# Two fused transformer blocks on one core: the modulation's loads and sums rearranged, the memory's keys and values moved beside the GLA projections, attention's last norms one step later

## The chip, the cores and the metric

The kernel runs on one core of a Trainium2 chip. TensorE (PE) multiplies matrices into PSUM banks; VectorE (DVE), ScalarE (ACT) and GpSimd (POOL) read and write SBUF and PSUM; 16 DMA engines move data between HBM and SBUF. Each engine executes its own list of instructions in order, and semaphores make one engine wait for another. The metric is the device time of one execution in microseconds (us); lower is better.

## The reference, cut to what matters

Two blocks run one after the other over a sequence of 1024 positions with 1024 channels, in fp32. The places that the change touches are the first norm and its modulation, the projections of gated linear attention (GLA), the keys and values of the cross-attention, and its last step with the norm behind it:

```python
# block 1
mod = silu(c) @ w_ada + b_ada                  # c: 1024 values, w_ada: 1024 x 6144
shift1, scale1, gate1, shift2, scale2, gate2 = split(mod, 6)
u = layer_norm(x) * (1 + scale1) + shift1      # x: 1024 x 1024
m = token_mixer(u, ...)                        # retention and GLA, w_in: 1024 x 3600
x = layer_norm(ALPHA*x + gate1*m, ...); u2 = layer_norm(x)*(1 + scale2) + shift2
x = layer_norm(ALPHA*x + gate2*(relu(u2 @ w_ff1)**2 @ w_ff2), ...)   # 4096 hidden channels
# block 2: a mixer of SSD, S5 and RG-LRU, then
k = mem @ wk; v = mem @ wv                     # mem: 256 x 1024, wk and wv: 1024 x 1024
o = softmax(q k^T / 16) v, 4 heads of 256; h = layer_norm(ALPHA*h1 + o @ wo, ln2)
# then an MLP with 4096 hidden channels and a last norm
```

## The kernel before, in words

The program is written as Python generators that are stepped beside each other: `weave(main, side, n)` steps `side` n times for each step of `main`, and `pipe` runs several generators one step behind each other. What they issue gets a fixed place on each engine at build time, so the order on every engine is set before the run.

**Products.** A matrix product in fp32 is made of three faster products (`mm3`, lines L114, L115, L116): each operand is kept as a rounded part `hi` (format fp32r) and the rest `lo`, and hi·hi, hi·lo and lo·hi are summed in PSUM. `split` makes the two parts: ACT casts (L82), DVE or POOL subtracts (L83). Weights are loaded into a staging page S and split into two pages each (`wpage`, `wcols`), with tag W by default. A page is 128 rows of 1024 values; there are U 4 (each four such pages wide), X 8, H 8, W 8, S 6.

**The start.** `kv_mem` transposes the two row tiles of `mem` on TensorE (L1080) and splits them into four X pages. `kv_proj` makes the cross-attention's keys (four steps of 256 columns, 48 products of 256 columns each) and values (two column halves, two steps each) and stores them to HBM; attention reads them some 1700 us later. `first_norm` loads x (four row tiles, then four more), normalises it, and has `mod_first` make scale1 and shift1: each needs eight row tiles of 128 x 1024 of w_ada. DVE adds six of them, each times its value of silu(c), into `acc` (L219, L221). TensorE then sums `acc` over its rows with one-column products against ones (L228, 8 of them), adds the last two row tiles directly (L230, 16 products against silu(c)), and DVE adds the bias (L233). Last, x is transposed on TensorE (L331, 64 transposes), scaled and shifted on the way out of PSUM, and split into the two parts of the page pair `T` (L341 subtracts). The main program steps `kv_proj` between the steps of `first_norm`, with POOL doing its weights' subtractions (`w_eng`).

**The GLA projections.** `gla_proj` reads T: 48 products give 16 gate channels, four fp32 products the gates (L404), then come four groups of 24 products of 512 columns for queries and four for keys (each copied out by ACT, L420), eight groups for values (ACT, L438) and eight for gates. Beside it, `early` makes the other four modulation vectors (`mods`: DVE sums w_ada tiles in X pages, in `mod_acc`, two of them summed by TensorE at L273 and finished by DVE at L274) and the constants of S5 (`s5_setup`, a long chain on DVE from L1420 on).

**The end of attention.** `attn_part(T, hd, h)` handles one head hd and one half h of the sequence in two steps: first queries, scores and the softmax, then the transposed probabilities (L1738), their product with the values, and the output projection added to the residual of each row tile. For the last head (hd == 3), each row tile is normalised at once, scaled (L171), stored as h2, transposed on TensorE (L182) and scaled and split for the MLP (ACT at L186). The MLP then starts with U pages as the left and W pages as the right operands; ACT finishes its first tiles at L772.

## Time and profile before

| | |
|---|---|
| three runs | 2683.71, 2690.9, 2692.58 us; median 2690.9 us |
| profiled execution | 2687.83 us, span of its trace 2686.1 us |
| mean granted clock of TensorE | 0.974 |
| TensorE busy | 2554.4 us, 95% of the span |
| VectorE, ScalarE, GpSimd busy | 1905.0, 1114.9 and 262.0 us (71%, 42%, 10%) |

The span is the stretch from the first to the last instruction that the trace holds; the rest of the execution's time lies around it. A busy time is the sum over one engine's instructions; TensorE's matrix products overlap in the records, so the distance from one start to the next is their real cost.

### The profile page before, as it was taken

Reading aid. Unit: us, or ns where it says so; the run is one execution under the profiler, and the core shown is the slowest. Engines: PE = TensorE matmul, PEld = TensorE weight load, DVE = VectorE, ACT = ScalarE, POOL = GpSimd, SP = SyncE. Lnnn points to the kernel's source line nnn. Section 1 sums busy time; section 2 is a strip of 40 time slices with the busy share of each in tenths; the row PEclk is TensorE's granted clock in tenths of the full one; section 3 lists DMA queues with packets and bytes.
Section 4 is the critical chain, followed back from the end, with each engine's and each line's share of the span. In section 5 each row is a group of like instructions: output and inputs, shape, how many; then the busy total and the mean of one; then the engine's idle time right before and its main releaser. Section 6 shows DMA issues by size and latency. Waiting matters only on the chain.

```text
span 2686.1 us, 32858 instructions
## 1 busy us (share of the span) xinstructions
PE 2554.4 (95%) x12086; PEld 2073.2 (77%) x12086; DVE 1905.0 (71%) x3237; ACT 1114.9 (42%) x1671; POOL 262.0 (10%) x238
## 2 busy tenths in 40 slices
PE   7899999889999999999999998999988999999997
PEld 7587777677888888888877776778867888888886
DVE  5858665778897777656965577785557787767759
ACT  3622233224654444433642572352246454434332
POOL 4121135530000000000001013100000000000000
PEclk8899999989999999999999998999998999999998
DMA  9772333454266568857632243361102756799763
GB/s 334 248 252 102 141 103 108 141 145 149 76 216 234 190 237 322 307 182 231 204 135 76 68 141 114 114 221 54 40 32 78 255 192 212 247 340 336 264 228 144
DMA packets 255129, 484.35 MB, mean 180 GB/s; under 512 B 21604, under 2 KB 110964, under 8 KB 254968
## 3 DMA queue, kind: packets, MB, share of 16 engines
q1 hardware_dynamic: 247768, 470.59, 51.7%
q10 hardware_dynamic: 7200, 11.67, 1.2%
q8 instruction: 95, 1.56, 0.2%
q14 instruction: 66, 0.54, 0.1%
HBM read 338.80 MB, written 143.38 MB: 180 GB/s over the span
## 4 chain that ended last, share of the span: by engine, by line
PE 75%; DVE 10%; ACT 4%; DMA 4%; issue 4%; POOL 3%; SPq 0%; POOLq 0%; DVEq 0%; ACTq 0%
PE ps L114 23%; PE ps L115 23%; PE ps L116 23%; ACT half L186 1%; DMA H<-r_qk 1%; PE ps L182 1%; DVE half L548 1%; DVE W L83 1%; DMA S<-in_xa_wk 1%; POOL X L527 1%; PE ps L540 1%; DVE st L155 1%; DMA H<-g_qkb 1%; POOL W L83 0%; DVE U L341 0%
## 5 line engine op out<-in xcount | busy, mean ns | idle before, releaser
L114 PE MATMUL ps<-U,W 128*128 128x512 f32 (+1 forms) x1080 | 426.1, 395 | 7.6 <-ACT ev L772 5.1
L114 PE MATMUL ps<-W,H 128*128 128x512 f32 x1088 | 425.1, 391 | 3.6 <-DVE sm L167 3.0
L115 PE MATMUL ps<-U,W 128*128 128x512 f32 (+1 forms) x1080 | 424.2, 393 | 1.5 <-DVE U L341 1.5
L115 PE MATMUL ps<-W,H 128*128 128x512 f32 x1088 | 423.9, 390 | 0.0
L116 PE MATMUL ps<-W,H 128*128 128x512 f32 x1088 | 423.9, 390 | 0.0
L83 DVE TENSOR_TENSOR W<-S,W 128x1024 fp32r<-128x1024 f32 (+1 forms) x272 | 330.2, 1217 | 131.6 <-ACT W L82 129.6
L116 PE MATMUL ps<-U,W 128*128 128x512 f32 (+1 forms) x1080 | 422.7, 392 | 0.8 <-DVE W L83 0.8
L82 ACT CAST W<-S 128x1024 fp32r<-128x1024 f32 x288 | 299.0, 1043 | 256.7 <-PE ps L115 175.6
L83 DVE TENSOR_TENSOR H<-S,H 128x1024 fp32r<-128x1024 f32 x130 | 158.5, 1220 | 154.2 <-ACT H L82 147.2
L82 ACT CAST H<-S 128x1024 fp32r<-128x1024 f32 x130 | 136.6, 1051 | 292.0 <-PE ps L115 226.1
L114 PEld LDWEIGHTS ps<-U,W 128*128 128x128 f32 (+1 forms) x1080 | 200.6, 186 | 57.5 <-ACT ev L772 5.4
L114 PEld LDWEIGHTS ps<-W,H 128*128 128x128 f32 x1088 | 204.7, 188 | 47.3 <-DVE X L1019 3.7
L115 PEld LDWEIGHTS ps<-U,W 128*128 128x128 f32 (+1 forms) x1080 | 200.7, 186 | 48.9 <-DVE U L341 4.6
L115 PEld LDWEIGHTS ps<-W,H 128*128 128x128 f32 x1088 | 204.7, 188 | 42.0
L116 PEld LDWEIGHTS ps<-W,H 128*128 128x128 f32 x1088 | 204.5, 188 | 42.3 <-DVE H L83 0.2
L116 PEld LDWEIGHTS ps<-U,W 128*128 128x128 f32 (+1 forms) x1080 | 200.5, 186 | 46.6 <-DVE W L83 1.9
L114 PE MATMUL ps<-W,U 128*128 128x512 f32 x352 | 142.7, 406 | 1.2 <-DVE X L274 0.8
L116 PE MATMUL ps<-W,U 128*128 128x512 f32 x352 | 141.3, 402 | 0.1
L115 PE MATMUL ps<-W,U 128*128 128x512 f32 x352 | 141.2, 401 | 0.0
L772 ACT ACTIVATE ev<-ev 128x512 f32<-128x512 f32 x104 | 65.5, 630 | 146.7 <-DVE ev L870 120.6
L1245 POOL TENSOR_TENSOR half<-tri,s_adt 128x512 f32<-128x512 f32 x16 | 19.7, 1244 | 890.3 <-DVE half L1123 778.8
L773 ACT ACTIVATE X<-ev 128x512 f32<-128x512 f32 x128 | 81.1, 636 | 3.5
(527 smaller groups left out, 4573.6 us busy)
## 6 DMA issues: line engine op xcount, KB each, us to landing
S<-mlp_h SPq DMA_DIRECT2D x112, 512.0 KB, 5.0
S<-in_w_ff SPq DMA_DIRECT2D x96, 512.0 KB, 5.1
mlp_h<-X SPq DMA_DIRECT2D x96, 512.0 KB, 4.1
S<-in_mlp_w SPq DMA_DIRECT2D x96, 512.0 KB, 4.9
mlp_w<-S SPq DMA_DIRECT2D x96, 256.0 KB, 2.6
S<-mlp_w SPq DMA_DIRECT2D x48, 512.0 KB, 4.7
S<-in_w_in SPq DMA_DIRECT2D x46, 512.0 KB, 5.7
X<-in_w_ada SPq DMA_DIRECT2D x32, 512.0 KB, 6.7
```

Source lines behind the costliest of these rows:

```text
L82: self.nc.scalar.copy(out=hi, in_=src)
L83: (lo_eng or self.nc.vector).tensor_tensor(out=lo, in0=src, in1=hi.bitcast(F32), op=ALU.subtract)
L114: mm(out=ps, lhsT=lh, rhs=rh, start=start and k == 0, stop=False)
L115: mm(out=ps, lhsT=lh, rhs=rl, start=False, stop=False)
L116: mm(out=ps, lhsT=ll, rhs=rh, start=False, stop=stop and k == n - 1)
L155: self.nc.vector.bn_stats(out=st[:, h, :], in_=y[:, h * 512:(h + 1) * 512])
L182: nc.tensor.transpose(ps[:, j * 128:(j + 1) * 128], y[:, k * 128:(k + 1) * 128], self.ident)
L186: nc.scalar.activation(out=full[:, j * 128:(j + 1) * 128], in_=ps[:, j * 128:(j + 1) * 128], func=ACTF.Identity, scale=scale[:, k:k + 1], ...
L527: nc.gpsimd.tensor_tensor(out=E[:, l, :].rearrange("p (g c) -> p g c", c=2 * w), in0=bv, in1=bv[:, :, w - 1:w].broadcast_to([128, 64 // w, ...
L540: nc.tensor.matmul(out=ps[:, r, u, :], lhsT=k[rs] if l < 0 else E[rs, l, :], rhs=q[rs] if l < 0 else qt[rs, l, :], start=True, stop=True)
L772: nc.scalar.activation(out=r, in_=x, func=ACTF.Relu)
L773: nc.scalar.activation(out=out, in_=r, func=ACTF.Square)
```

## The change

It has three parts. First, `mod_load` issues the loads of w_ada before anything else waits for them: four tiles of x, eight tiles for scale1, four tiles of x, eight for shift1. In `mod_first`, TensorE sums the first four of the eight row tiles directly (L227 in the changed kernel, 32 one-column products), DVE the last four (L220 and three times L222), TensorE sums DVE's result over its rows into a second PSUM tile (L231, 8 products), and DVE adds it (L236) to what it made of the first (L234). `first_norm` is no generator any more; every second instead of every fourth transposed piece goes through ACT alone.

Second, the memory's transposes and the keys and values stand after the first norm, as the first part of `early`: two steps of it run ahead of `gla_proj`, the rest beside it, with 0.9 instead of 0.75 side steps for each main step. The weights' parts now lie in X pages (of which `mem` holds four, so four are left: one set of weights), DVE does the subtractions, and the values come in four steps of 256 columns.

Third, in the last head's `attn_part` the norms, the store of h2 and the transposes come behind another `yield`: one step later, for all four row tiles together.

```diff
@@ -206,32 +206,34 @@
         self.silu_c = sc
         self.mod = {}
 
-    def mod_first(self, j, name, plus):
-
-        nc = self.nc
+    def mod_load(self, j):
         w = [self.page("U", F32, [128, 4, 1024]) for _ in range(2)]
-        KD = 6
-        acc = w[0][:, 0, :]
         for k in range(8):
-            nc.sync.dma_start(out=w[k // 4][:, k % 4, :],
-                              in_=self.I["w_ada"][128 * k:128 * k + 128, j * 1024:(j + 1) * 1024])
...
+            self.nc.sync.dma_start(out=w[k // 4][:, k % 4, :],
+                                   in_=self.I["w_ada"][128 * k:128 * k + 128, j * 1024:(j + 1) * 1024])
+        return w
+
+    def mod_first(self, w, j, name, plus):
+
+        nc = self.nc
+        acc = w[1][:, 0, :]
+        nc.vector.tensor_scalar(out=acc, in0=acc, scalar1=self.silu_c[:, 4:5], scalar2=None, op0=ALU.mult)
+        for k in range(1, 4):
+            nc.vector.scalar_tensor_tensor(out=acc, in0=w[1][:, k, :], scalar=self.silu_c[:, 4 + k:5 + k], in1=acc,
+                                           op0=ALU.mult, op1=ALU.add)
         ps = self.ps("tr")
         for f in range(8):
-            fs = slice(128 * f, 128 * f + 128)
...
+            for k in range(4):
+                nc.tensor.matmul(out=ps[:, f:f + 1], lhsT=w[0][:, k, 128 * f:128 * f + 128], rhs=self.silu_c[:, k:k + 1],
+                                 start=k == 0, stop=k == 3)
+        pa = self.ps("tr")
+        for f in range(8):
+            nc.tensor.matmul(out=pa[:, f:f + 1], lhsT=acc[:, 128 * f:128 * f + 128], rhs=self.ones[:, 0:1], start=True,
+                             stop=True)
...
+        nc.vector.tensor_tensor(out=m, in0=pa[:, 0:8], in1=m, op=ALU.add)
         self.mod[name] = m
 
     def mod_acc(self, j):
@@ -315,23 +317,23 @@
                 nc.sync.dma_start(out=xs[t], in_=x[t * 128:(t + 1) * 128, :])
 
         load()
-        yield
-        self.normalize4(xs)
-        yield from self.mod_first(1, "scale1", 1.0)
-        yield from self.mod_first(0, "shift1", 0.0)
+        wa = self.mod_load(1)
         load()
+        wb = self.mod_load(0)
+        self.normalize4(xs[:4])
+        self.mod_first(wa, 1, "scale1", 1.0)
+        self.normalize4(xs[4:])
+        self.mod_first(wb, 0, "shift1", 0.0)
         T = self.new_T()
         sc, sh = self.mod["scale1"], self.mod["shift1"]
         for h in range(2):
-            if h:
-                self.normalize4(xs[4:])
             for k in range(8):
...
-                if k % 4 == 3:
+                if k % 2:
...
@@ -339,9 +341,7 @@
...
-                if k % 2:
-                    yield
-        yield T
+        return T
 
 
 
@@ -1087,7 +1087,7 @@
         self.kd = self.dram([D, 256], "kT")
         self.vd = self.dram([256, D], "v")
         for c in range(4):
-            W = self.wcols(I["xa_wk_2"], 256 * c, 256)
+            W = self.wcols(I["xa_wk_2"], 256 * c, 256, tags="X")
...
@@ -1096,16 +1096,16 @@
                 nc.scalar.copy(out=o[:, 0:256], in_=ps[:, 0:256])
                 nc.scalar.dma_start(out=_rows(self.kd, 2 * c + m), in_=o[:, 0:256])
             yield
-        for n in range(2):
-            W = self.wcols(I["xa_wv_2"], 512 * n, 512)
+        for c in range(4):
+            W = self.wcols(I["xa_wv_2"], 256 * c, 256, tags="X")
             for t in range(2):
                 ps = self.ps()
                 sl = slice(128 * t, 128 * t + 128)
-                self.mm3(ps, [(a[:, sl], b[:, sl]) for a, b in mk], W)
+                self.mm3(ps[:, 0:256], [(a[:, sl], b[:, sl]) for a, b in mk], W)
                 o = self.ev()
-                nc.scalar.copy(out=o, in_=ps)
-                nc.scalar.dma_start(out=self.vd[128 * t:128 * t + 128, 512 * n:512 * n + 512], in_=o)
-                yield
+                nc.scalar.copy(out=o[:, 0:256], in_=ps[:, 0:256])
+                nc.scalar.dma_start(out=self.vd[128 * t:128 * t + 128, 256 * c:256 * c + 256], in_=o[:, 0:256])
+            yield
 
     def log1p(self, e, n):
 
@@ -1761,9 +1761,11 @@
                 ps = self.ps("sc")[:, 0:512]
                 self.mm3(ps, [(oh[:, m, ts], ol[:, m, ts]) for m in range(2)], [(a[:, 0, c], b[:, 0, c]) for a, b in Wo])
                 self.add_res(acc[t][:, c], ps, hd == 0)
-            if hd == 3:
-                if t == 0:
-                    st8["T"] = self.new_T()
+        if hd == 3:
+            yield
+            if h == 0:
+                st8["T"] = self.new_T()
+            for t in range(4 * h, 4 * h + 4):
                 self.normalize(acc[t], acc[t], True)
                 nc.sync.dma_start(out=_rows(self.h2d, t), in_=acc[t])
                 self.to_T(acc[t], t, st8["T"], self.pvec("ln2_g_2"), self.pvec("ln2_b_2"))
@@ -1796,7 +1798,6 @@
     with ExitStack() as ctx:
         n = Mix2(tc, ctx, I, out)
         n.modulation()
-        n.kv_mem()
...
@@ -1809,21 +1810,17 @@
                 yield
             yield from g
 
-        norm, kv = n.first_norm(I["x"]), n.kv_proj()
-        T, steps = None, [3, 0, 1, 0, 1]
-        while T is None:
-            n.w_eng = n.nc.gpsimd
-            for _ in range(steps.pop(0) if steps else 1):
-                next(kv, None)
-            n.w_eng = n.nc.vector
-            T = next(norm)
-        run(kv)
+        T = n.first_norm(I["x"])
+
         def early():
-            for _ in range(3):
-                yield
+            n.kv_mem()
+            yield from n.kv_proj()
             yield from n.mods()
             yield from n.s5_setup()
-        run(n.weave(n.gla_proj(T), early(), 0.75))
+        side = early()
+        for _ in range(2):
+            next(side)
+        run(n.weave(n.gla_proj(T), side, 0.9))
         n.gla_setup()
         run(n.weave(n.ret_proj(T), n.pipe(n.gla_block(i) for i in range(NB)), 0.3))
         n.ret_setup()
```

The fixed order of the engines shows what moved. At the start, TensorE had the transposes of `mem` (ident is the identity, H a page of `mem`) and the first key products (X and W, mm3 lines) first; these are its first rows before:

```order
L1080 MATMUL ps_94<-ident,H_92 128x128 x4
L1080 MATMUL ps_101<-ident,H_92 128x128 x4
L1080 MATMUL ps_110<-ident,H_108 128x128 x4
L1080 MATMUL ps_117<-ident,H_108 128x128 x4
L114 MATMUL ps_138<-X_88,W_127 128x256
L114 MATMUL ps_166<-X_88,W_127 128x256
L115 MATMUL ps_138<-X_89,W_127 128x256
```

After, on the same engine and place, the modulation's one-column products (U is a page of w_ada) and the transposes of x (L333, H a tile of x) stand first, and those of `mem` follow behind all 64 of them:

```order
L227 MATMUL ps_161<-silu_c,U_96 128x1 x32
L231 MATMUL ps_194<-ones,U_97 128x1 x8
L227 MATMUL ps_243<-silu_c,U_114 128x1 x32
L231 MATMUL ps_276<-ones,U_115 128x1 x8
L333 MATMUL ps_292<-ident,H_88 128x128
L333 MATMUL ps_292<-ident,H_90 128x128
```

VectorE's part of the first modulation vector, after (ps_161 holds the 32 products, ps_194 the 8; cv is the bias):

```order
L234 SCALAR_TENSOR_TENSOR scale_203<-ps_161,cv 128x8
L220 TENSOR_SCALAR U_97<-U_97,silu_c 128x1024
L222 SCALAR_TENSOR_TENSOR U_97<-U_97,silu_c 128x1024 x3
L236 TENSOR_TENSOR scale_203<-ps_194,scale_203 128x8
L301 BN_STATS st_207<-H_106 128x6 x2
L302 BN_AGGR sm_206<-st_207 128x2
```

The instruction that reads TensorE's 32 products stands ahead of the sums that VectorE makes itself. The norm of x's second half follows, and then the same five rows for shift1, with L234 ahead of its sums there too.

Where the first group of GLA queries (U is T, W its weights, ps_981) begins, TensorE has, before, behind the gates:

```order
L404 MATMUL ps_944<-H_880,half_933 128x512
L404 MATMUL ps_955<-H_880,half_933 128x512
L404 MATMUL ps_959<-H_880,half_933 128x512
L114 MATMUL ps_981<-U_613,W_969 128x512
L115 MATMUL ps_981<-U_614,W_969 128x512
L116 MATMUL ps_981<-U_613,W_970 128x512
```

After, the same group (ps_785) stands between the keys' third and fourth step (left operand X, 256 columns), here its beginning:

```order
L114 MATMUL ps_744<-X_438,X_711 128x256
L115 MATMUL ps_744<-X_439,X_711 128x256
L116 MATMUL ps_744<-X_438,X_712 128x256
L114 MATMUL ps_785<-U_288,W_773 128x512
L115 MATMUL ps_785<-U_289,W_773 128x512
L116 MATMUL ps_785<-U_288,W_774 128x512
```

All six steps of keys and values stood ahead of this group; now three of eight do. Its end on the same engine, after:

```order
L114 MATMUL ps_785<-U_288,W_779 128x512
L115 MATMUL ps_785<-U_289,W_779 128x512
L116 MATMUL ps_785<-U_288,W_780 128x512
L114 MATMUL ps_824<-X_436,X_813 128x256
L115 MATMUL ps_824<-X_437,X_813 128x256
L116 MATMUL ps_824<-X_436,X_814 128x256
```

Of the other five steps one follows each group; the last stands behind the fifth group.

At the end of attention TensorE transposed, before, the normalised tiles of the first half (L182, X pages) around the probabilities of the second (L1738):

```order
L116 MATMUL ps_16032<-W_15712,H_15731 128x512
L182 MATMUL ps_15884<-ident,X_14547 128x128 x4
L182 MATMUL ps_15896<-ident,X_14547 128x128 x4
L1738 MATMUL ps_16082<-ident,half_15819 128x128 x4
L1738 MATMUL ps_16082<-ident,half_15839 128x128 x4
L182 MATMUL ps_15942<-ident,X_14569 128x128 x4
L182 MATMUL ps_15954<-ident,X_14569 128x128 x4
L182 MATMUL ps_16000<-ident,X_14591 128x128 x4
L182 MATMUL ps_16012<-ident,X_14591 128x128 x4
L182 MATMUL ps_16058<-ident,X_14613 128x128 x4
L182 MATMUL ps_16070<-ident,X_14613 128x128 x4
L114 MATMUL ps_16097<-H_16091,bc_15541 128x512
```

After, the probabilities and their product with the values (H and bc pages) follow at once:

```order
L116 MATMUL ps_16046<-W_15856,H_15875 128x512
L1738 MATMUL ps_16054<-ident,half_15963 128x128 x4
L1738 MATMUL ps_16054<-ident,half_15983 128x128 x4
L114 MATMUL ps_16069<-H_16063,bc_15685 128x512
L114 MATMUL ps_16078<-H_16063,bc_15685 128x512
L115 MATMUL ps_16069<-H_16064,bc_15685 128x512
```

The 32 transposes of the first half now stand among the output projection of the second half (left operand W, right operand H), from its third product on.

## Rows read from the trace of the kernel before

**Rows 1.** The page's head: span, and busy time, share and instructions of each engine.
```profile
span 2686.1 us, 32858 instructions
PE 2554.4 (95%) x12086; PEld 2073.2 (77%) x12086; DVE 1905.0 (71%) x3237; ACT 1114.9 (42%) x1671; POOL 262.0 (10%) x238
```

**Rows 2.** Windows: start:end, us; PE, PEld, DVE, ACT, POOL busy; PEclk, DMA share, GB/s.
```profile
0.00:131.30 131.30, 109.37 (x545) 84.54 (x546) 87.20 (x119) 63.85 (x80) 42.16 (x20) 0.86 0.84 291
```

**Rows 3.** ACT's timeline (start, us, instruction, idle before), first and fifth group of GLA.
```profile
131.31 0.60 ACT L420 ACTIVATE ev<-ps 128x512 f32<-128x512 f32 x1 [1.23 <-PE ps L116]
...
153.07 0.60 ACT L420 ACTIVATE ev<-ps 128x512 f32<-128x512 f32 x1 [4.12 <-DMA X<-in_w_ada]
```

**Rows 4.** PE's timeline, 209 to 214 us, the modulation's row sums.
```profile
210.18 1.87 PE L273 MATMUL ps<-bc,ones 128*1 128x512 f32 x2 [2.92 <-ACT ev L438]
...
213.59 0.80 PE L114 MATMUL ps<-W,U 128*128 128x512 f32 x1 [0.83 <-DVE X L274]
```

**Rows 5.** The same windows view, end of attention.
```profile
1997.90:2055.60 57.70, 40.20 (x185) 31.32 (x183) 36.08 (x101) 43.73 (x93) 0.00 (x0) 0.83 0.18 73
```

**Rows 6.** ACT's timeline, end of attention and start of the MLP.
```profile
1997.90 1.24 ACT L171 ACTIVATE X<-X,sm,sm 128x1024 f32<-128x1024 f32 x1 [7.32 <-DVE sm L170]
...
2033.62 1.05 ACT L82 CAST W<-S 128x1024 fp32r<-128x1024 f32 x1 [10.13 <-PE ps L115]
...
2055.63 0.78 ACT L772 ACTIVATE ev<-ps 128x512 f32<-128x512 f32 x1
```

**Rows 7.** PE's timeline, start of the MLP's unbroken products.
```profile
2056.47 0.80 PE L114 MATMUL ps<-U,W 128*128 128x512 f32 x1 [5.12 <-ACT ev L772]
```

**Rows 8.** DMA, 0 to 60 us in 40 slices of 1.5 us: GB/s moved.
```profile
GB/s 0 145 230 382 369 376 350 349 346 347 397 415 396 415 401 419 424 363 325 45 109 348 329 350 338 412 425 350 270 326 322 314 391 397 209 215 371 330 358 374
```

**Rows 9.** PE's timeline, 72 to 77 us: one-column products, then the first transposes.
```profile
72.26 0.58 PE L230 MATMUL ps<-silu_c,U 128*128 128x1 f32 x4
72.71 0.36 PE L228 MATMUL ps<-ones,U 128*128 128x1 f32 x2
72.93 0.99 PE L230 MATMUL ps<-silu_c,U 128*128 128x1 f32 x4
73.78 1.95 PE L331 MATMUL ps<-ident,H 128*128 128x128 f32 x8
76.88 0.90 PE L331 MATMUL ps<-ident,H 128*128 128x128 f32 x3 [1.15 <-DVE half L339]
```

**Rows 10.** Windows of PE: start:end, us; busy (instructions), PEclk, DMA share, GB/s.
```profile
50.00:52.00 2.00, 2.00 (x20) 1.00 0.89 325
52.00:54.00 2.00, 2.00 (x14) 0.62 0.76 191
...
209.50:219.70 10.20, 8.70 (x18) 0.50 0.07 27
```

**Rows 11.** DVE's timeline, sums of the first modulation vector.
```profile
25.24 0.74 DVE L219 TENSOR_SCALAR U<-U,silu_c 128x1024 f32<-128x1024 f32 x1
...
28.43 2.60 DVE L221 SCALAR_TENSOR_TENSOR U<-U,silu_c 128x1024 f32<-128x1024 f32 x2
```

**Rows 12.** PE's timeline: first transposes of mem, first products, two later ones, gates.
```profile
6.57 1.94 PE L1080 MATMUL ps<-ident,H 128*128 128x128 f32 x8 [6.57 <-DMA H<-in_mem]
...
10.85 0.58 PE L114 MATMUL ps<-X,W 128*128 128x256 f32 x1
...
19.27 0.28 PE L114 MATMUL ps<-X,W 128*128 128x256 f32 x1
19.63 0.28 PE L114 MATMUL ps<-X,W 128*128 128x256 f32 x1
...
121.82 2.07 PE L404 MATMUL ps<-H,half 16*128 16x512 f32 x2 [0.15 <-DVE H L406]
```

**Rows 13.** DVE's timeline, first and last link of the S5 constants' chain.
```profile
201.14 0.17 DVE L1420 COPY s5p<-bc 128x24 f32<-128x24 f32 x1
...
228.53 1.22 DVE L1371 TENSOR_TENSOR bc<-bc,bc 128x1024 f32<-128x1024 f32 x1
```

More of the change, by code (lines that the diff above doesn't have):

```diff
@@ L207, in modulation @@
         self.mod = {}
-    def mod_first(self, j, name, plus):
-        nc = self.nc
-        w = [self.page("U", F32, [128, 4, 1024]) for _ in range(2)]
-        KD = 6
-        acc = w[0][:, 0, :]
-        for k in range(8):
-            nc.sync.dma_start(out=w[k // 4][:, k % 4, :],
-                              in_=self.I["w_ada"][128 * k:128 * k + 128, j * 1024:(j + 1) * 1024])
-            if k == 0:
-                nc.vector.tensor_scalar(out=acc, in0=acc, scalar1=self.silu_c[:, 0:1], scalar2=None, op0=ALU.mult)
-            elif k < KD:
-                nc.vector.scalar_tensor_tensor(out=acc, in0=w[k // 4][:, k % 4, :], scalar=self.silu_c[:, k:k + 1], in1=acc,
-                                               op0=ALU.mult, op1=ALU.add)
-            if k % 4 == 3:
-                yield
+    def mod_load(self, j):
+        w = [self.page("U", F32, [128, 4, 1024]) for _ in range(2)]
+        for k in range(8):
+            self.nc.sync.dma_start(out=w[k // 4][:, k % 4, :],
+                                   in_=self.I["w_ada"][128 * k:128 * k + 128, j * 1024:(j + 1) * 1024])
+        return w
@@ L228, in mod_first @@
-            nc.tensor.matmul(out=ps[:, f:f + 1], lhsT=acc[:, fs], rhs=self.ones[:, 0:1], start=True, stop=False)
-            for k in range(KD, 8):
-                nc.tensor.matmul(out=ps[:, f:f + 1], lhsT=w[1][:, k - 4, fs], rhs=self.silu_c[:, k:k + 1], start=False,
-                                 stop=k == 7)
+            for k in range(4):
+                nc.tensor.matmul(out=ps[:, f:f + 1], lhsT=w[0][:, k, 128 * f:128 * f + 128], rhs=self.silu_c[:, k:k + 1],
+                                 start=k == 0, stop=k == 3)
@@ L333, in first_norm @@
                 hi, lo = T[h][0][:, k, :], T[h][1][:, k, :]
-                if k % 4 == 3:
+                if k % 2:
                     nc.scalar.activation(out=full, in_=ps, func=ACTF.Identity, scale=sc[:, k:k + 1], bias=sh[:, k:k + 1])
@@ L1810, in delay @@
             yield from g
-        norm, kv = n.first_norm(I["x"]), n.kv_proj()
-        T, steps = None, [3, 0, 1, 0, 1]
-        while T is None:
-            n.w_eng = n.nc.gpsimd
-            for _ in range(steps.pop(0) if steps else 1):
-                next(kv, None)
-            n.w_eng = n.nc.vector
-            T = next(norm)
-        run(kv)
+        T = n.first_norm(I["x"])
         def early():
-            for _ in range(3):
-                yield
+            n.kv_mem()
+            yield from n.kv_proj()
             yield from n.mods()
             yield from n.s5_setup()
-        run(n.weave(n.gla_proj(T), early(), 0.75))
+        side = early()
+        for _ in range(2):
+            next(side)
+        run(n.weave(n.gla_proj(T), side, 0.9))
         n.gla_setup()
```

## The prediction

> **What bounds the kernel now.** First the page's head: TensorE is busy for 2554.4 of 2686.1 us [rows 1]. No other engine comes near, so a change helps only where it fills one of the gaps that are left (some 130 us in all), and it costs where it opens one. Two places of the change have gaps. The first is the start, read from the windows: in the first 131.3 us TensorE is busy for 109.37 [rows 2]. From there on the groups of the GLA projections follow each other closely: ACT copies the first out at 131.31 and the fifth at 153.07, (153.07 - 131.31)/4 = 5.44 us for each group of 24 products, 0.227 us for one [rows 3]. At 153 all keys and values are done. So 153.07 with all keys, all values and five groups is the point of equal work at which I compare the two versions. Some 57 us later there is a smaller gap: TensorE waits 2.92 us at the modulation's row sums and 0.83 behind them [rows 4], and runs at half clock from 209.5 to 219.7 with 8.70 us busy [rows 10]. The second place is the end of attention. In the 57.70 us up to 2055.60, ACT is busy for 43.73 and TensorE for 40.20 [rows 5]. ACT's timeline shows why neither is full: it waits 7.32 us for a norm's sums, then 10.13 us for TensorE [rows 6], which stands behind transposes that need the same norms; TensorE's free run begins only at 2056.47, after 5.12 us of waiting for ACT's copy at 2055.63 [rows 6, 7]. The two engines take turns there.
>
> **The start, step by step.** The chain of loads comes first. TensorE's first product needs the constants, four tiles of x and four of w_ada: 0.26 + 2.1 + 2.1 = 4.5 MB. By the slices of moved bytes, 4.4 MB have landed after ten slices of 1.5 us [rows 8], so it can start at 15.0 us. Nothing stands ahead of it that would use the time before, where the old order had the transposes of mem from 6.57 and products from 10.85 [rows 12].
>
> The one-column products have two prices. Where they follow without a break, each shows as two records. Six records from 72.26 to 72.93 give 0.223 us a product, four from 72.93 to 73.78 give 0.425 [rows 9]. These are the two clock levels, 2.4 and 1.2 GHz: the clock was 1.00 at 50 to 52, during an unbroken series of them, and 0.62 in the next two [rows 10]. So in the old kernel such a series ran down a clock that was up. Here TensorE comes to the series from idle, and I take 0.425: 32 products 13.6 us, 8 products 3.4 (7.1 and 1.8 at full clock).
>
> The order on VectorE lets nothing overlap with the 32: the instruction that reads them (L234) stands ahead of the four sums. One sum costs 0.74 us, and the others 2.60 for two records of one instruction each, 1.3 apiece [rows 11]: 0.74 + 3 x 1.3 = 4.6. So scale1: 15.0 + 13.6 = 28.6; the sums to 33.2; 8 products to 36.6. The loads for shift1 (12.6 MB with all that stands ahead, at some 0.37 MB a us [rows 8] about 34 us) are there by then. Shift1: TensorE's next 32 products wait for nothing but the first 8, to 50.2; sums to 54.8; 8 products to 58.2; the addition to 58.5. The norm of x's second half fills VectorE while it would wait anyway. Then come the transposes of x. A pair of pieces took from 73.78 to 76.88, 3.1 us, of which 1.95 is TensorE [rows 9]; with a half instead of a quarter of the pieces on ACT I take 3.0 for each of 8 pairs, 24 us, to 82.5. The old kernel had only begun with them by then [rows 9], so up to here the new order is far ahead. But it has done nothing else.
>
> Next on TensorE stand mem's transposes and the first keys' products, before at 6.57 and 10.85, 4.3 us apart [rows 12]; with the weight's split I take 4.8, to 87.3. Two key steps are 96 products of 256 columns; two products of the same kind that stand three apart began at 19.27 and 19.63, 0.12 each [rows 12]: 11.4 us, and some 4.3 for a start at half clock and the second step's weights, which need the same four X pages: to 103.0. The 48 products for the gate channels take 48 x 0.227 = 10.9, to 113.9. The gates follow: two products 2.07 [rows 12], four 4.1, with 1.8 for their waits, to 119.8. The third key step (48 x 0.12 = 5.7) to 125.5, the first group of queries (5.44) to about 131, where the old kernel was as well. But then three of the eight steps are done, not all. The order puts one of the other five beside each of the following groups; their casts and subtractions have a group's 5.44 us as cover, and without it each would add some 2 us. So 5 x 5.7 = **28.5 us behind**. That is also what the gaps say: TensorE does the same products in either version, and idles here for 15 us at first and for two times 4.6 and most of 8 x 1.1 later, and crawls through 80 one-column products where 48 stood before.
>
> **What is given back near 210.** The modulation's other vectors come later (the X pages are free only when the last value step is done), their row sums are no longer in the way, and 2.92 + 0.83 us of waits go [rows 4]. The half clock, which the wait brought, goes as well: 8.70 us busy at 0.50 is 4.3 too many [rows 10]. Together **-8**. Late next is the chain of the S5 constants, 201.14 to 228.53 [rows 13], which moves behind the row sums; the transposes that need it may wait for 0 to 5 us, and I take **+1**. The lag is then 21.5.
>
> **The end of attention.** The norms of the first half now run while TensorE does the second half's probabilities and output projection. ACT starts with the cast of the probabilities, about 1.7 us into the old stretch, at 1999.6, and has the same 43.7 us of work in front of the MLP [rows 5]. With 2.5 us of waits for VectorE it comes to the copy of 2055.63 at about 2045.8: **-9.8**. The bounds are -13 (of ACT's 14 idle us only 1 is left) and -6 (8 us of idle stay, as VectorE's 36.08 us of work [rows 5] come in one bunch for each half).
>
> **Sum.** 2687.8 + 28.5 - 8 + 1 - 9.8 = 2699.5, rounded 2700. The profiled execution's 2687.8 stands 3 us under the median of the three runs.
>
> **The rivals.** *The clock comes up* (B). Eighty one-column products in nearly one row could raise the clock, as other work did at 50 us. Against it stands that it fell during such a series twice [rows 9, 10]. If it did rise, the two vectors would take 2 x (6.5 + 1.6) = 16.2 us less, and 8 pairs of transposes, with TensorE's 1.95 us in each halved, some 7 less: 23 off, 2677, faster than before. From half of that on (11 to 12 off, 2688) the whole change is no loss. The Trainium skill ("TensorE: Matmul & The Clock Gate", "What's actually happening") has the clock follow how busy TensorE has been of late; by that rule an unbroken series should bring it up and the time would be the 2677 of this rival. The trace has the contrary at 52 to 54 us, 0.62 behind 1.00 [rows 10], so I trust the row.
>
> *Attention gains nothing* (C). ACT has the same work, and if it waits as long as before, only elsewhere (the cast of the probabilities stands in front, and VectorE bunches four norms), the end stays where it is: 2700 + 9.8 = 2710. For it speaks that ACT and VectorE together were busy for 80 of 2 x 57.7 us [rows 5]; against it, that the 10.13 us wait [rows 6] is for products which wait for norms no more.
>
> *The lag is partly absorbed* (D). The projections could run with fewer gaps than I count in front (4.3 and 1.8 us), S5's chain could wait for nothing and the transposes could be shorter with more pieces on ACT; then some 10 us of the 28.5 go, 2690, no change.
>
> **How the numbers follow.** The forecast has 0.55, with 2693 to 2707 as its own range (-6 to -13 in attention, 0 to 5 at S5, some 3 us either way in front). B has 0.15, C 0.10, D 0.20. A measurement of this kernel tells about 0.3%, 8 us, from no change. Slower by more than that means above 2696 (by the profiled run): most of the forecast (0.41 of 0.55) and C, 0.51. Faster is B alone, 0.15. D and the low end of the forecast are the same, 0.34. For 8 in 10 the range runs from B's 2677 to C's 2709.
>
> **What would show it.** The 32 products (L227) take 13 to 14 us each at a granted clock of 0.50; scale1 is ready at about 37, shift1 at 58; the last transpose of x ends near 83; the first key products start near 87; ACT's first copy of a query group stands at about 131 with five steps of keys and values behind it, the last value's copy near 182. The wait of 2.92 us at the row sums is gone. Between the last attention head's products and ACT's first MLP copy lie some 10 us less. The prediction is wrong if the granted clock is 1.00 in most of 20 to 80 us, if mem's loads or the weights' splits leave gaps of several us between the steps beside the groups, or if the stretch at the end of attention keeps its 57.7 us.

## The result: slower by 0.8%

The changed kernel takes 2710.73 us in the median of four runs (2707.76 to 2713.85), the kernel before 2691.74 (2683.71 to 2692.71). The ratio is 1.0081, with a 95% interval of 1.0061 to 1.0101. The forecast was slower, 2700 us, and its range ended at 2709: the way was right, the size too small by 11 us and just out of the range.

The page of the changed kernel's profile, span and busy times; TensorE does the same sums, with 32 more one-column products and the values made by twice as many products of half the width (160 records more in all), in a span that is 19.5 us longer [rows 1]:

```profile
span 2705.6 us, 33210 instructions
PE 2566.3 (95%) x12246; PEld 2093.7 (77%) x12246; DVE 1904.8 (70%) x3247; ACT 1123.0 (42%) x1681; POOL 215.0 (8%) x222
```

The same windows view of the start as in [rows 2]; TensorE is busy for 97.09 us in place of 109.37:

```profile
0.00:131.30 131.30, 97.09 (x470) 80.44 (x471) 66.48 (x114) 54.93 (x70) 0.20 (x4) 0.97 0.54 189
```

TensorE's timeline at the start (start, duration, instruction, idle before it and what ended it):

```profile
16.08 12.53 PE L227 MATMUL ps<-silu_c,U 128*128 128x1 f32 x58 [0.69 <-DMA U<-in_w_ada]
33.49 3.58 PE L231 MATMUL ps<-ones,U 128*128 128x1 f32 x16 [4.88 <-DVE U L222]
36.92 13.79 PE L227 MATMUL ps<-silu_c,U 128*128 128x1 f32 x64
55.69 3.55 PE L231 MATMUL ps<-ones,U 128*128 128x1 f32 x16 [4.97 <-DVE U L222]
59.10 1.95 PE L333 MATMUL ps<-ident,H 128*128 128x128 f32 x8
...
86.09 0.50 PE L114 MATMUL ps<-X,X 128*128 128x256 f32 x2
```

The reader sees the forecast chain piece by piece: 32 products in 13.8 us (64 records; forecast 13.6), a wait of 4.9 for VectorE's sums, 8 products in 3.5, the same again, then the transposes from 59.10 (forecast 58.5), and the first key products at 86.09 (forecast 87.3). ACT's copies of the GLA groups (L420) and of the last value step (L1106):

```profile
130.81 0.60 ACT L420 ACTIVATE ev<-ps 128x512 f32<-128x512 f32 x1 [3.58 <-PE ps L116]
...
175.66 0.60 ACT L420 ACTIVATE ev<-ps 128x512 f32<-128x512 f32 x1 [4.25 <-PE ps L116]
...
181.42 0.37 ACT L1106 COPY ev<-ps 128x256 f32<-128x256 f32 x1 [2.50 <-PE ps L116]
```

The first group is copied out from 130.81 (131.31 before [rows 3]), but the point of equal work, 153.07 before [rows 3], is now 181.42: 28.35 us behind, forecast 28.5. From here on the two traces can be laid beside each other, since the instructions are the same. First TensorE at a step of the first GLA block, before and after (the second view ends inside the step, so it counts fewer of its 24 records):

```profile
302.67 1.61 PE L540 MATMUL ps<-X,X 64*128 64x128 f32 x24
```

```profile
334.68 1.50 PE L540 MATMUL ps<-X,X 64*128 64x128 f32 x22
```

Then ACT just ahead of the change in attention, before and after:

```profile
1974.86 0.59 ACT L82 CAST H<-ps 128x512 fp32r<-128x512 f32 x1 [3.61 <-PE ps L116]
```

```profile
2005.21 0.59 ACT L82 CAST H<-ps 128x512 fp32r<-128x512 f32 x1 [3.61 <-PE ps L116]
```

And ACT at the end of attention, after: the cast of the last head's probabilities and the MLP's first copies:

```profile
2029.34 1.01 ACT L82 CAST H<-ps 128x1024 fp32r<-128x1024 f32 x1 [8.43 <-PE ps L1738]
...
2074.88 1.26 ACT L772 ACTIVATE ev<-ps 128x512 f32<-128x512 f32 x2
```

So the changed kernel is 28.35 us behind at the end of the keys and values, 32.0 behind in the first GLA block (334.68 - 302.67), 30.35 ahead of attention, and 19.25 at the MLP's first copy (2074.88 against 2055.63 [rows 6]): attention gave 11.1. The two large terms came as forecast. What did not come is the gain between 200 and 300 us: forecast 7, measured a loss of 3.65.

TensorE's waits of over a microsecond between 240 and 300 us, after (the kernel before has none from 214 to 309 us):

```profile
255.43 0.49 PE L540 MATMUL ps<-X,X 64*128 64x128 f32 x4 [1.57 <-POOL X L533]
...
270.98 0.50 PE L114 MATMUL ps<-W,U 128*128 128x512 f32 x1 [1.37 <-DVE ev L436]
...
284.90 1.07 PE L1500 MATMUL ps<-ident,bc 128*128 128x128 f32 x8 [2.61 <-DVE bc L1371]
...
288.46 1.94 PE L1500 MATMUL ps<-ident,bc 128*128 128x128 f32 x8 [2.27 <-DVE bc L1374]
```

The windows view of TensorE for two stretches behind these waits, one behind the first and one from the third on (busy, granted clock, DMA share, GB/s):

```profile
256.60:260.10 3.50, 3.47 (x9) 0.52 0.64 197
287.30:294.20 6.90, 5.74 (x18) 0.51 0.48 177
```

VectorE at both ends of the chain that ends in the first of L1500's operands, after:

```profile
235.04 0.17 DVE L1420 COPY s5p<-bc 128x24 f32<-128x24 f32 x1
...
283.54 1.22 DVE L1371 TENSOR_TENSOR bc<-bc,bc 128x1024 f32<-128x1024 f32 x1
```

The waits of [rows 4] are indeed gone. But there are four new ones of 7.8 us in all, and half of the 3.47 and 5.74 us at half clock, 4.6 us, comes on top: 12.4 lost for the 8 regained. Two of the four waits (4.88 us) are for the operands that S5's chain makes, one is for GpSimd and one for VectorE's copy of the gates. The chain of S5's constants, 27.4 us long before [rows 13], took 48.5.

### The profile page after: what moved, and what is told of

Same layout as the page of the kernel before. It is cut to its first block, busy times and chain, and to the rows that moved or that the text cites. A ratio compares the mean times of both kernels' runs of the same rounds, so it can differ in the third digit from the quotient of the medians.

```text
span 2705.6 us, 33210 instructions
## 1 busy us (share of the span) xinstructions
PE 2566.3 (95%) x12246; PEld 2093.7 (77%) x12246; DVE 1904.8 (70%) x3247; ACT 1123.0 (42%) x1681; POOL 215.0 (8%) x222
## 4 chain that ended last, share of the span: by engine, by line
PE 66%; DVE 6%; ACT 3%; issue 1%; POOL 1%; DMA 0%; SPq 0%; POOLq 0%; DVEq 0%; ACTq 0%
PE ps L114 21%; PE ps L115 21%; PE ps L116 21%; ACT half L186 1%; PE ps L182 1%; DVE W L83 0%; DVE X L1043 0%; DVE X L1044 0%; DVE bc L1181 0%; DVE st L155 0%; PE ps L1638 0%; PE ps L1264 0%; ACT U L82 0%; DVE U L83 0%; PE ps L1672 0%
## 5 line engine op out<-in xcount | busy, mean ns | idle before, releaser
L83 DVE TENSOR_TENSOR W<-S,W 128x1024 fp32r<-128x1024 f32 (+1 forms) x272 | 330.8, 1218 | 127.8 <-ACT W L82 127.4
L82 ACT CAST W<-S 128x1024 fp32r<-128x1024 f32 (+1 forms) x272 | 282.9, 1044 | 252.4 <-PE ps L115 174.0
L83 DVE TENSOR_TENSOR H<-S,H 128x1024 fp32r<-128x1024 f32 x130 | 158.8, 1221 | 149.7 <-ACT H L82 144.4
```

The lines of the kernel that those rows point to most:

```text
L82: self.nc.scalar.copy(out=hi, in_=src)
L83: (lo_eng or self.nc.vector).tensor_tensor(out=lo, in0=src, in1=hi.bitcast(F32), op=ALU.subtract)
```

## The experiments

The changes of the runs are against the kernel before or after, as named; each was timed in alternation with the kernel before. "Under the changed kernel" compares the medians with 2710.7. The median of the kernel before lay between 2689.4 and 2691.7 in the groups of runs, so such a difference is good to some 2 us.

**Attention alone (e1_attn_only).** The kernel before with the last head's norms one step later:

```diff
-            if hd == 3:
-                if t == 0:
-                    st8["T"] = self.new_T()
+        if hd == 3:
+            yield
+            if h == 0:
+                st8["T"] = self.new_T()
+            for t in range(4 * h, 4 * h + 4):
                 self.normalize(acc[t], acc[t], True)
```

> The kernel before with the third part of the change alone: the last head's norms, store and transposes one step later. My account of the changed kernel's trace (A): the lag is 30 us ahead of attention and 19 behind it, so this part gives 11 us and the start costs 30. Then this run is 11 us under the kernel before (ratio 0.996), and the stretch from the last attention head's output projection to the MLP's free run is 10 to 11 us shorter. Rival (B): the later norms give nothing, as ACT has the same work, and the start costs 19. Then this run stays within 2 us of the kernel before.

Measured: 2678.68 us against 2689.63, ratio 0.9959 (0.9946 to 0.9971), 11 us faster. TensorE's free run in the MLP, at 2056.47 before [rows 7], begins here at

```profile
2045.92 0.79 PE L114 MATMUL ps<-U,W 128*128 128x512 f32 x1 [5.13 <-ACT ev L772]
```

10.55 us earlier. This part of the change is a gain of its own, and the start costs some 30.

**The start alone (e2_front_only).** The changed kernel with the lines above put back.

> The changed kernel with attention's norms where they were before: the first two parts of the change alone. A: 30 us over the kernel before (ratio 1.011), 11 over the changed kernel. B: as the changed kernel, 19 us over the kernel before (1.007). Either way the copy of the fifth GLA group and of the last value step stand at 175 to 182 us.

Measured: 2721.32 us, ratio 1.0116 (1.0102 to 1.0130), 31.7 us over the kernel before. The two parts add: 31.7 - 11.0 = 20.7, measured together 19.0. The rival that attention gives nothing is out. Up to attention this run has the changed kernel's order, and its trace repeats it: 153.3 us from the last value step's copy to the GLA block's step in either.

**The transposes of S5 one step later (e3_s5_one_step_later).** The changed kernel with

```diff
         G = outer(Bb, dre, dim, 0)
         yield
+        yield
         self.s5_G = self.dram([128, 2, 1024], "s5_G")
```

> The changed kernel with one more yield between S5's first two outer products and the transposes that read them, so that one more group of 24 products stands ahead of the transposes on TensorE. If the part of the gain near 210 that did not come is the wait of these transposes for VectorE (2.6 and 2.3 us) and the half clock that it brought, both go: 7 to 8 us under the changed kernel, and the granted clock stays 1.00 from 285 to 300 us. Rival: VectorE is behind with everything by then (mods' sums and S5's chain and the first GLA block), so the time is lost at another wait a step later; then this is within 2 us of the changed kernel.

Measured: 2709.33 us, ratio 1.0068 (1.0055 to 1.0081), 1.4 under the changed kernel, which the intervals don't tell apart. In the trace the waits at the transposes are gone and the clock is 1.00 from 287.3 to 294.2, but another wait for VectorE stands a group later, at the copy of the gates (the view of the GLA step ends inside it, here and in the next run):

```profile
281.79 0.50 PE L114 MATMUL ps<-W,U 128*128 128x512 f32 x1 [1.38 <-DVE ev L436]
...
327.62 0.60 PE L540 MATMUL ps<-X,X 64*128 64x128 f32 x6
```

The step of the first GLA block is 7.1 us ahead of the changed kernel's 334.68; some 2 of that it had already brought from the start, so the edit gave 5 there. By the end the profiled execution had lost all of it. The expectation held for the place and fell for the end.

**S5's chain ahead of the other modulation vectors (e11_s5_chain_first).** The changed kernel with

```diff
             yield from n.kv_proj()
+            s5 = n.s5_setup()
+            next(s5)
+            yield
             yield from n.mods()
-            yield from n.s5_setup()
+            yield from s5
```

> The changed kernel with the first step of S5's setup, the long chain of small VectorE instructions, ahead of the other modulation vectors instead of behind them (a yield after it; the outer products and the transposes stay where they were). In the changed kernel this chain took from 235.0 to 283.5 us, with the four additions of the row sums and the first GLA block between its links, where the kernel before had 201.1 to 228.5. If it is the chain's late start that took back the gain near 210 (waits of 2.6 and 2.3 us at the transposes, and half clock behind them), the transposes wait for nothing, TensorE stands 5 to 8 us ahead of the changed kernel at 340 us, and the end comes 3 to 8 us earlier. Rival: it is the sum of VectorE's work between 200 and 290 us; then the waits come back at the row sums or at the gates' copies, and the run is within 2 us of the changed kernel.

Measured: 2704.99 us, ratio 1.0061 (1.0047 to 1.0075), 5.7 under the changed kernel; the times of the two overlap (2704.4 to 2710.3 against 2707.8 to 2713.9), so the end alone doesn't settle it, and the trace has to. VectorE's first link stands at 68.4 us. ACT's copy of the last value step comes first here, then TensorE: the transposes wait for nothing; one wait stands at the row sums, where the rival had it:

```profile
183.25 0.37 ACT L1106 COPY ev<-ps 128x256 f32<-128x256 f32 x1 [2.50 <-PE ps L116]
...
268.38 1.02 PE L275 MATMUL ps<-bc,ones 128*1 128x512 f32 x2 [2.19 <-DVE ev L436]
269.33 0.76 PE L1500 MATMUL ps<-ident,bc 128*128 128x128 f32 x5
...
326.77 0.49 PE L540 MATMUL ps<-X,X 64*128 64x128 f32 x4
```

The clock is full in the two stretches that ran at half in the changed kernel:

```profile
256.60:260.10 3.50, 3.50 (x17) 1.00 0.15 47
287.30:294.20 6.90, 6.90 (x32) 1.00 0.21 54
```

At the GLA block's step TensorE stands at 326.77, 7.9 us ahead of the changed kernel, although it was 1.8 behind at the last value's copy (183.25 against 181.42). It needs 143.5 us for this stretch, the changed kernel 153.3 and the kernel before 149.6 (302.67 - 153.07): 9.7 us won by the edit, and 6.1 gained on the kernel before, where 7 had been forecast. Both numbers, 7.9 and 5.7, lie in the expectation for the late chain, not in the rival's 2 us. One thing moved with the chain: the four products that waited for GpSimd at 255.43 stand in the later GLA step here (28 records in place of 24), so some of the 9.7 may be theirs.

**VectorE's own sums first (e4_sums_first).** The changed kernel with the two additions swapped, so that the one which reads TensorE's 32 products comes last:

```diff
-        nc.vector.scalar_tensor_tensor(out=m, in0=ps[:, 0:8], scalar=plus, in1=self.pvec("b_ada")[:, 8 * j:8 * j + 8],
+        nc.vector.scalar_tensor_tensor(out=m, in0=pa[:, 0:8], scalar=plus, in1=self.pvec("b_ada")[:, 8 * j:8 * j + 8],
                                        op0=ALU.add, op1=ALU.add)
-        nc.vector.tensor_tensor(out=m, in0=pa[:, 0:8], in1=m, op=ALU.add)
+        nc.vector.tensor_tensor(out=m, in0=ps[:, 0:8], in1=m, op=ALU.add)
```

> The changed kernel with the two last additions of each modulation vector swapped: VectorE first reads the PSUM tile of its own sums' 8 products, then that of the 32, so that its four sums no longer stand behind TensorE's 32 products. If the chain of 32 products, sums and 8 products is what sets the start, both waits of 4.9 us of TensorE go and all behind moves 9 to 10 us ahead, to 2701. Rival: the loads or ACT's copies of the transposed pieces set the start's end, or the time is given back at 210 to 310 us where VectorE is late; then 0 to 4 us less.

Measured: 2705.31 us, ratio 1.0056 (1.0042 to 1.0070), 5.4 under the changed kernel. All five times lie under the changed kernel's four. The end keeps only some 5 us, between the expectation (9 to 10) and its rival (0 to 4), although the first GLA group is copied out earlier by the 9.6 us expected, and TensorE's waits for the sums are gone:

```profile
27.96 3.55 PE L231 MATMUL ps<-ones,U 128*128 128x1 f32 x16
45.44 3.55 PE L231 MATMUL ps<-ones,U 128*128 128x1 f32 x16
49.35 1.94 PE L333 MATMUL ps<-ident,H 128*128 128x128 f32 x8 [0.35 <-DVE shift L234]
```

**All sums on VectorE (e5_all_dve).** The changed kernel without the 32 products:

```diff
-        acc = w[1][:, 0, :]
+        acc = w[0][:, 0, :]
...
-        for k in range(1, 4):
+        for k in range(1, 8):
...
-        for f in range(8):
-            for k in range(4):
-                nc.tensor.matmul(out=ps[:, f:f + 1], lhsT=w[0][:, k, 128 * f:128 * f + 128], rhs=self.silu_c[:, k:k + 1],
-                                 start=k == 0, stop=k == 3)
```

> The changed kernel with all eight row tiles of each modulation vector summed by VectorE and only the 8 products against ones left to TensorE. If TensorE's 2 x 32 one-column products at 0.43 us each and their place in one chain with VectorE's sums are what makes the start long, the transposes of x begin at 44 to 48 us in place of 59, 11 to 15 us ahead; by the run with the sums first, about half to two thirds of that is left at the end: 6 to 10 us under the changed kernel. Rival: VectorE's sums (0.74 + 7 x 1.3 us for each vector) and the norm of x's second half on the same engine take as long as TensorE's products did; then 0 to 3 us.

Measured: 2701.17 us, ratio 1.0047 (1.0033 to 1.0060), 9.6 under the changed kernel. TensorE waits for VectorE here, and is still earlier: the transposes begin 11.8 us ahead of 59.10.

```profile
23.27 3.57 PE L226 MATMUL ps<-ones,U 128*128 128x1 f32 x16 [23.27 <-DVE U L222]
43.90 3.57 PE L226 MATMUL ps<-ones,U 128*128 128x1 f32 x16 [17.05 <-DVE U L222]
47.33 1.95 PE L327 MATMUL ps<-ident,H 128*128 128x128 f32 x8
```

Yet the first GLA group is copied out at 120.80, hardly ahead of e4's 121.20, where TensorE still made its 32 products. So in front it is the place of the sums behind these products that cost some 10 us, and not the products by themselves; at the end e5's median is 4.1 us under e4's, and their intervals overlap.

**Two key steps ahead (e6_kv_ahead).** The changed kernel with the order of two pieces turned round:

```diff
-        T = n.first_norm(I["x"])
-
...
         for _ in range(2):
             next(side)
+        T = n.first_norm(I["x"])
```

> The changed kernel with mem's transposes and the first two key steps ahead of the first norm, as they were in the kernel before; the other six steps stay beside the GLA projections. If the start costs because TensorE has nothing to do until x and w_ada have landed, it works from some 7 us on and the gate channels' products are done some 10 us earlier (at about 100 us in place of 110.7), although the loads of w_ada stand some 8 us later: 5 to 10 us under the changed kernel at the end. Rival: every load in front delays the chain of the modulation by as much as it fills; then no change within 3 us.

Measured: 2693.70 us, ratio 1.0016 (1.0007 to 1.0024), 17.0 under the changed kernel, more than expected. The timeline of TensorE shows a second effect:

```profile
27.11 9.57 PE L227 MATMUL ps<-silu_c,U 128*128 128x1 f32 x64
41.66 3.55 PE L231 MATMUL ps<-ones,U 128*128 128x1 f32 x16 [4.97 <-DVE U L222]
45.07 14.04 PE L227 MATMUL ps<-silu_c,U 128*128 128x1 f32 x64
...
77.86 1.04 PE L333 MATMUL ps<-ident,H 128*128 128x128 f32 x8
```

The windows view of the two series of 32 products has the granted clock (0.74 and 0.50):

```profile
27.10:36.60 9.50, 9.50 (x66) 0.74 0.98 362
45.00:59.00 14.00, 13.92 (x65) 0.50 0.96 320
```

Behind the key products the clock was up, and the first series took 9.57 us; during it the clock fell, and the second took 14.04. Later the gate channels' products stand among the transposes, the clock comes up again, and eight transpose records take 1.04 us in place of 1.95. The first GLA group is copied out at 112.47, 18.3 us ahead of the changed kernel.

**Both, and four steps (e7_both, e8_both4).** e7 has the edits of e5 and e6; e8 has four key steps in place of two, and the extra yield of e3.

> Both of these edits in one kernel. If idle time of TensorE in front and the one-column products are two separate costs, their gains add, and more, since the transposes of x then overlap with the gate channels' products: the gate channels' products are done at 80 to 88 us in place of 110.7, and the end comes 15 to 25 us before the changed kernel's, some 2690. Rival: one hides the other; then no better than the better of the two by 3 us.

Measured: 2686.24 us, ratio 0.9990 (0.9981 to 0.9999), 24.5 under the changed kernel: 9.6 + 17.0 = 26.6 nearly add.

> The same with four key steps in place of two ahead of the first norm, and with the extra yield in S5's setup. Two more steps are 11.4 us of products that need no GLA weights and cost some 5 us of loads in front. If TensorE still waits for the modulation in the run with two, they are nearly free: 5 to 10 us under that run, 2680 or less, as fast as the kernel before with the attention part alone (2678.7). Rival: the loads push the modulation back by what they fill: within 3 us of it.

Measured: 2675.48 us, ratio 0.9951 (0.9938 to 0.9963), 10.8 under e7. The edit has two parts (steps and yield), which this run doesn't tell apart. TensorE still waits for both vectors, longest for the second:

```profile
43.91 3.55 PE L226 MATMUL ps<-ones,U 128*128 128x1 f32 x16 [3.51 <-DVE rs L147]
63.82 3.54 PE L226 MATMUL ps<-ones,U 128*128 128x1 f32 x16 [16.36 <-DVE U L222]
```

**All eight steps ahead (e9_all8, e10_all8_pool).** e8 with `range(8)`; e10 also with `n.w_eng = n.nc.gpsimd` during these steps.

> The run with four key steps ahead, but with all eight steps of keys and values ahead of the first norm. In that run TensorE still waited 3.5 and 16.4 us for the two modulation vectors; four more steps are 4 x 5.9 us of products. If the cost of the change was work taken out of these waits, they fill them, and x's transposes begin no more than 5 us later than there (67 us) while 23.6 us of products are gone behind them: 12 to 18 us under that run, 2658 to 2664, faster than the kernel before and than its attention part alone. Rival: the four more MB of loads push the modulation back by their own 11 us and the weights' splits load VectorE: 2670 to 2676, no better.

Measured: 2677.69 us, ratio 0.9952 (0.9939 to 0.9965): no better than e8, as the rival has it (its 2670 to 2676 were still too low). The transposes begin at 83.67 in place of 67.22, and the first GLA group is copied out at 131.30, where the kernel before stood too.

> The same with the weights' subtractions of these eight steps on GpSimd, as they were in the kernel before, so that VectorE only sums and normalises in front. If VectorE's splits hold up the modulation, this is 3 to 6 us faster than the run with all eight on VectorE; if loads or TensorE set the pace there, the two are the same within 2 us, or GpSimd's slower subtractions make it up to 5 us slower.

Measured: 2688.65 us, ratio 0.9991 (0.9979 to 1.0002), 11 slower than e9. The waits of TensorE show where: before x's transposes begin it waits 5.8 us for VectorE's subtractions of the weights (L83) in e9, and 14.3 for GpSimd's in e10, and the first GLA group is copied out at 142.55, 11.3 us later. The relief of VectorE does not make up for that; this is beyond the 5 us that I allowed.

Three versions beat the kernel before: e1, e8 and e9, by 0.4 to 0.5% (e7's 0.1% is at the edge of its interval). Their intervals don't tell them apart; e1 is much the smallest edit. Since e8 and e9 have the attention part too, which is worth 0.4% alone, their rearranged starts are no clear gain over the old start.

## Why the prediction was right and wrong

**The start** came as worked out: the first products at 12.36 in small pieces and in full from 16.08 (forecast 15.0), 13.8 and 3.5 us for the series, transposes from 59.10, the equal point 28.35 behind. The choice of 0.425 us for a one-column product was right. The prediction named a granted clock of 1.00 between 20 and 80 us as a sign of being wrong, and the clock's view does say 1.00 for all of 15 to 90 us, because no change of clock is on record in this run before the first key products; the products' own pace tells more, and e6 has the same pace (14.04 us for 32) with 0.50 on record beside it. That the first GLA group came within 0.2 us of the forecast is partly luck: the gate channels' products ended some 3 us early, at 110.98 (forecast 113.9), and a stretch at half clock behind them (0.50 from 113.6 to 117.5), which the prediction didn't have, took that back. e4 and e5 add the reason for the long start: with VectorE's sums no longer behind TensorE's 32 products (e4), or without these products (e5), the first GLA group comes 9.6 or 10.0 us earlier. So it is the order on VectorE, as the prediction had it.

**The rival "the clock comes up"** fell: no series of one-column products raised the clock, and in e6 it fell in the middle of one. The rule that was cited for it (the Trainium skill, "TensorE: Matmul & The Clock Gate", "What's actually happening") speaks of how busy the engine has been; here an unbroken series of one-column products, at 9.50 us busy of 9.50, did not hold the clock, so the row decides.

**What is given back near 210** is the step that failed. The prediction had "Together -8" and for S5's chain "I take +1", with a bound of 5. The waits and the half clock of the kernel before did go: counted by the GLA projections' products on TensorE (left operand W, right operand U), the changed kernel is 28.35 us behind at the equal point and 19.3 behind at 227 us of the old trace. (Of these 9 us, 1.9 are only the first row sums, which stand further back now.) Then the lag grows again, to 32.0 from 286 us of the old trace on.

The "+1" is the term that failed. The chain was taken over with its old length, 27.4 us, and only its start was moved; it took 48.5. Its own links took 26.8 us (23.5 before), the instructions that now stand between them on VectorE 14.1 (3.5 before: additions of the row sums, weights' splits, the first GLA block, gates), and waits 7.6 (0.4), of which 4.4 is the first addition's for TensorE's row sums. At the transposes the waits came to 4.88 us, just inside the bound of 5; what had no term at all is the half clock behind them (2.9), and the other two waits with the half clock behind the first (4.7). e11 shows the cause: with the chain ahead of the modulation vectors, the same step of the GLA block stands 7.9 us earlier, the stretch up to it is 9.7 shorter, and the clock stays full; at the end 5.7 are left, with the times overlapping. How much of the 4.7 is the chain's doing stays open, since e11 moved the GLA block's four products too. e3 shows that pushing only the reader back moves part of the loss to the next reader of VectorE's work.

**Attention** came as worked out: -9.8 forecast, -11.1 in the profiled pair, -11.0 by e1 alone. (The bound of -13 left out the 1.7 us by which ACT starts later; with them it is -11.3.)

**The sum** with the measured terms: 2687.8 + 28.35 + 3.65 - 1.65 (between the first GLA block and attention) - 11.1 = 2707.05; the profiled execution took 2707.76. Against this execution the forecast of 2699.5 is 8.3 short, and the term near 210, with +3.65 in place of -7, is 10.65 by itself; the front, attention and the stretch between make up for some of it. The other 3 us of the miss are the base: the sum starts from an execution that lies 3.9 under the kernel's median of 2691.74, the changed kernel's profiled one lies 3.0 under its own. From the median the measured time would have been inside the range, and the term near 210 just as wrong.

What stays open: of 9.6 us gained in front, e4 kept 5.4 at the end, e11's profiled execution kept 3 of its 7.9, and e3 lost all of its 5. In the traces the loss lies in the retention blocks, the SSD blocks and attention, where stretches of half clock stand at other places than in the changed kernel. e2 has the same order as the changed kernel up to attention, and still stood 2 to 4 us behind it from the retention blocks to S5's mixer, with 0.5 before and after. That these differences come from the clock's stretches is argued, not shown.

## What to carry to other kernels

A chain of work that is moved on an in-order engine need not keep its length: here the new neighbours between its links, and their waits, took it from 27.4 to 48.5 us, so cost the chain anew from the order of the changed kernel. A first load that everything waits for is best covered by products that need little: here two to four key steps in front were worth more than loading x and w_ada first. And try the parts of a change apart: one of the three was a gain of 0.4%, hidden under a loss of 1.2%.

## What the runs showed of the hardware

One-column fp32 products did not hold TensorE's clock although they followed without a break: 0.223 us each at full clock [rows 9], 0.43 at half, and in e6 the clock fell from one to the other within 32 of them. Eight transpose records of x took 1.95 us in the changed kernel, where nothing else stood among them, and 1.04 in e6 from the fourth eight on, where the gate channels' products of 512 columns did. Two of the small instructions of S5's chain took 2.10 us each on VectorE in place of 0.17 (at 261.27 and 267.87 of the changed kernel's trace), both beside a GpSimd instruction of 2.1 us (L533).
